# Keys' weights behind the first loads, x scaled on VectorE, block products' weights at shifting offsets

## Chip, core and metric

The kernel runs on one NeuronCore of a Trainium2 chip. The metric is the device time of one execution in microseconds, taken as the median of several runs. TensorE multiplies matrices, VectorE and ScalarE do the elementwise work, GpSimd does a little of it and issues some transfers, and SP (SyncE) issues the other transfers. Each engine works through its own instructions in order.

## Reference

One layer of a hybrid decoder on x of 512 x 1024 float32: a token mixer (HGRN2 and gated DeltaNet side by side, 4 heads of 128) and a SwiGLU feed-forward part.

```python
def hybrid_layer(x, ...):
    u = rms_norm(x, pre_mix_w)
    proj = u @ w_in                       # 512 x 6152
    hg_q, hg_f, hg_i, hg_g, dn_q, dn_k, dn_v, dn_g, dn_a, dn_b, m_a, m_b = split(proj)
    o_a = head_rms_norm(hgrn2_mix(hg_q, hg_f, hg_i, lb), hg_norm_w) * silu(hg_g)
    cq, ck, cv = split(silu(causal_short_conv(concat(dn_q, dn_k, dn_v), conv_w)))
    o_b = head_rms_norm(gated_deltanet_mix(cq, ck, cv, dn_a, dn_b, ...), dn_norm_w) * silu(dn_g)
    merged = sigmoid(m_a) * (o_a @ w_o_hg) + sigmoid(m_b) * (o_b @ w_o_dn)
    h = x + rms_norm(merged @ w_out, post_mix_w)
    gate, up = split(rms_norm(h, pre_ffn_w) @ w_gate_up)      # 2 x 2816
    return h + rms_norm((silu(gate) * up) @ w_down, post_ffn_w)
```

## The kernel before

Every operand of a large product is split into a high part (cast to float32r by ScalarE) and a low part (the rest, a subtraction), and a product is three matmuls: high by high, high by low, low by high. Weights come from memory through `wload`: a transfer of 512 KB on SP's queue into one of two buffers `raw`, a cast on ScalarE into one of three buffers `whi` (L114), a subtraction on VectorE into one of three buffers `wlo` (L115). `wload` runs at high priority.

The order of each engine's instructions is made by a planner, ahead of the run, from priorities and the times that it expects. `high_priority` moves instructions ahead; `issue_after(ins)` puts the instructions of its block behind `ins` where they are on the same engine.

`start` (L195 to L268) comes first. Nine matmuls on a matrix of ones warm TensorE up (L202). Then eight pieces of x transposed (`xT`, L211, 256 KB each) and eight pieces of the weights `w_iab` (L217, 260 KB each) are loaded in pairs, with four pieces of x in rows (L228, 512 KB each) between them. ScalarE multiplies a piece of x by the gains `pmw` into its high part (L218), VectorE makes the low part (L155); the weights are split by a cast (L126) and a subtraction (L152). From these come 192 matmuls (L251) with 256 or 264 columns. The first product uses x before its normalisation; the normalising factor of each token is applied afterwards, and as a row vector, copied to all partitions, it is `rbc` (L267).

`mixers` (L756) follows. The keys' projection `dn_k` (four `wload`s, 96 matmuls of 512 columns, L122 and L123) also uses the unnormalised operand. `normalise` (L270) makes the operands of all later projections: a GpSimd product of x and `rbc` (L277), a ScalarE activation with the gains (L278), a VectorE operation for the low part (L279). Each head of the keys passes a short convolution on VectorE (`conv_evac`). `gates` makes small tables and sends them through memory by GpSimd's queue. Then comes `hg_f`, the forget gate's projection, the first that reads the normalised operand; the column sums of the keys (L392, L393) are set between its matmuls.

The feed-forward part makes 14 of its 22 column blocks by seven half-size products each (`winograd`, `product`, L1086 to L1088): 84 matmuls of 256 columns a block, with moving operands made once and weights made by `operand` from sums of weight blocks. Two such weights share one buffer of `whi` and one of `wlo`, one in each half. `out_proj` and the down projection work with 512 columns.

The tag `st` has three buffers. They hold the states of the two recurrences, then the two halves of `pre_ffn_w` (L918), then those of `post_ffn_w` (L1213). Their loads are on GpSimd's queue, which also carries the stores of the merge gate `m_a` (`early_a`, L826).

Of the kernel before, what the change touches and what calls it, by code (L numbers as in the profile page):

```python
# [9 lines left out]
F32 = mybir.dt.float32  # L10
F32R = mybir.dt.float32r
BF16 = mybir.dt.bfloat16
U32 = mybir.dt.uint32
AF = mybir.ActivationFunctionType
ALU = mybir.AluOpType

P = 128
# [4 lines left out]
NH = 4  # L22
# [2 lines left out]
EPS = 1e-6  # L25
NEG = -30000.0
FIRST, PACE = 8, 5
PADS = (96, 48)
HG_LEVELS = (64, 32, 16, 8, 4, 2, 1)
HG_MASKS = (16, 8, 4, 2, 1)  # L30

# [14 lines left out]
class K:  # L46
    def __init__(self, ctx, nc, tc, I, out):
        self.nc, self.tc, self.I, self.out = nc, tc, I, out
        e = ctx.enter_context
        self.cp = e(tc.tile_pool(name="cp", bufs=1))  # L50
        self.wp = e(tc.tile_pool(name="wp", bufs=1))
        self.bp = e(tc.tile_pool(name="bp", bufs=1))
        self.tp = e(tc.tile_pool(name="tp", bufs=1))
        self.dp = e(tc.tile_pool(name="dp", bufs=1, space=bass.MemoryType.DRAM))
        self.ps = e(tc.tile_pool(name="ps", bufs=1, space=bass.MemoryType.PSUM))
        self.n = self.ncol = self.nraw = 0
        self.log = {}


# [16 lines left out]
        return self.tp.tile([P, 512], F32, tag="out", name=self.name("out"), bufs=1)  # L76

    def st(self):
        return self.tp.tile([P, NH, P], F32, tag="st", name=self.name("st"), bufs=3)

    def sm(self, shape, bufs=1):
        nm = self.name("sm")
# [22 lines left out]
    def wload(self, src, shape):  # L105

        nc = self.nc
        n = shape[1] * shape[2]
        with self.tc.high_priority():
            raw = self.wp.tile([P, 1024], F32, tag="raw", name=self.name("raw"), bufs=2)  # L110
            hi = self.wp.tile([P, 1024], F32R, tag="whi", name=self.name("whi"), bufs=3)
            lo = self.wp.tile([P, 1024], F32R, tag="wlo", name=self.name("wlo"), bufs=3)
            nc.sync.dma_start(out=raw[:, :n], in_=src)
            nc.scalar.copy(hi[:, :n], raw[:, :n])  # L114
            nc.vector.tensor_tensor(out=lo[:, :n], in0=raw[:, :n], in1=hi[:, :n].bitcast(F32),  # L115
                                    op=ALU.subtract)
        r = lambda t: t[:, :n].rearrange("p (a b) -> p a b", a=shape[1])
        return r(hi), r(lo)

    def mm3(self, ps, lh, ll, rh, rl, start, stop):  # L120
        mm = self.nc.tensor.matmul
        return [mm(ps, lh, rh, start=start, stop=False), mm(ps, lh, rl, start=False, stop=False),  # L122
                mm(ps, ll, rh, start=False, stop=stop)]  # L123
# [34 lines left out]
    def consts(self):  # L158
        nc, I = self.nc, self.I
        nc.scalar.preload_act_table_set("natural_log_exp_and_others")  # L160

        self.pads = [self.cp.tile([P, n], F32, name=f"pad{i}") for i, n in enumerate(PADS[:1])]
        self.onesr = self.cp.tile([P, P], F32R, name="onesr")
        self.first = nc.vector.memset(self.onesr.bitcast(F32), 1.0)

        ncm = 3 + len(HG_MASKS)
        self.cm = self.cp.tile([P, ncm, P], F32, name="cm")
        self.ident, self.triu, self.negm = (self.cm[:, i, :] for i in range(3))
        self.hgm = {h: self.cm[:, 3 + i, :] for i, h in enumerate(HG_MASKS)}
        self.one = self.cp.tile([P, 1], F32, name="one")  # L170
        nc.vector.memset(self.one, 1.0)
        self.eps = self.cp.tile([P, 1], F32, name="eps")
        nc.vector.memset(self.eps, EPS)
        self.lnqs = self.cp.tile([P, 1], F32, name="lnqs")
        nc.vector.memset(self.lnqs, -0.5 * math.log(128.0))
        self.pmw = self.cp.tile([P, KD], F32, name="pmw")
        nc.gpsimd.dma_start(out=self.pmw, in_=I["pre_mix_w"])
        self.pads.append(self.cp.tile([P, PADS[1]], F32, name="pad1"))
        self.cw = self.cp.tile([P, 12, 4], F32, name="cw")
        self.hnw = self.cp.tile([P, 1], F32, name="hnw")  # L180
        self.dnw = self.cp.tile([P, 1], F32, name="dnw")
        self.albc = self.cp.tile([P, 2, 4], F32, name="albc")
        self.lbraw = self.cp.tile([P, 4], F32, name="lbraw")

# [10 lines left out]
    def start(self):  # L195

        nc, I = self.nc, self.I
# [9 lines left out]
        pw = lambda k: self.pmw[:, k:k + 1]  # L207
        for k in range(KD):
            g, j = k // 4, k % 4
            x_, h_, l_ = xr[g][:, j, :], uhi[g][:, j, :], ulo[g][:, j, :]  # L210
            nc.sync.dma_start(out=x_, in_=I["xT"][k])  # L211

            if k % 3 == 0:
                W = [self.slot(j, [P, 3, 640], dt)
                     for j, dt in zip(((15, 0, 3), (4, 1, 13), (15, 2, 14))[k // 3], (F32, F32R, F32R))]
            raw, hi, lo = (w[:, k % 3, :520] for w in W)
            nc.sync.dma_start(out=raw, in_=I["w_iab"][k // 2, :, k % 2 * 520:k % 2 * 520 + 520])  # L217
            A.activation(h_, x_, AF.Copy, scale=pw(k))  # L218
            self.stt(l_, x_, pw(k), h_.bitcast(F32), ALU.mult, ALU.subtract)
            self.split(hi, lo, raw)  # L220
            ws.append((hi, lo))
            if k == 3:
                nc.sync.dma_start(out=self.cm[:, 0:1], in_=I["cmat"][:, 0:1])
            if k >= 3 and k < 7:
                c = k - 3
                if c % 2 == 0:
                    xt.append(self.slot(11 + c // 2, [P, 2, D]))
                nc.sync.dma_start(out=xt[-1][:, c % 2, :], in_=I["x"][c])  # L228
# [14 lines left out]
        for k in range(KD):  # L243
            wh, wl = ws[k]
            st, sp = k == 0, k == KD - 1
            for c in range(NC_):
                ts = slice(c * P, c * P + P)
                uh, ul = uhi[k // 4][:, k % 4, ts], ulo[k // 4][:, k % 4, ts]
                for o, ns, s0 in ((pa[c // 2][:, c % 2 * 256:c % 2 * 256 + 256], slice(0, 256), c % 2 == 0),
                                  (pb[c][:, :264], slice(256, 520), True)):  # L250
                    mm = lambda l, r, **kw: nc.tensor.matmul(o, l, r, skip_group_check=True, **kw)  # L251
                    mm(uh, wh[:, ns], start=st and s0, stop=False)
                    mm(uh, wl[:, ns], start=False, stop=False)
                    mm(ul, wh[:, ns], start=False, stop=sp)
# [15 lines left out]
    def normalise(self):  # L270

        self.xhi = [self.slot(i, [P, 4, S], F32R) for i in range(2)]
        self.xlo = [self.slot(2 + i, [P, 4, S], F32R) for i in range(2)]
        for k in range(KD):
            g, j = k // 4, k % 4
            x, h, pw = self.xr[g][:, j, :], self.xhi[g][:, j, :], self.pmw[:, k:k + 1]
            self.tt(x, x, self.rbc, ALU.mult, self.nc.gpsimd)  # L277
            self.nc.scalar.activation(h, x, AF.Copy, scale=pw)  # L278
            self.stt(self.xlo[g][:, j, :], x, pw, h.bitcast(F32), ALU.mult, ALU.subtract)  # L279


    def small_hg(self):
# [473 lines left out]
    def mixers(self):  # L756
        nc = self.nc
# [1 line left out]
        cm = lambda t: (lambda h, ps: A.copy(t[:, :, h, :], ps.rearrange("p (c t) -> p c t", c=NC_)))  # L759
        run = lambda g: [None for _ in g]  # L760
        self.kT = self.slot(11, [P, NH, S])
        self.dense_in("dn_k", self.conv_evac(self.kT, 4, self.rbc), self.u)
        self.normalise()
        with self.tc.issue_after(self.lasta.ins), self.tc.issue_after(self.lastv.ins):
            self.gates()
# [48 lines left out]
        for c in range(NC_):  # L814
            n = self.dn_step(c)
# [46 lines left out]
        for c in range(NC_):  # L862
# [3 lines left out]
            n = self.hg_step(c, at[c])  # L866
# [122 lines left out]
    def operand(self, src):  # L989

        if self.half is None:
            self.half = [self.wp.tile([P, 1024], F32R, tag=t, name=self.name(t), bufs=3) for t in ("whi", "wlo")]
            o = [t[:, :512] for t in self.half]
        else:
            o = [t[:, 512:1024] for t in self.half]
            self.half = None
        self.split(o[0], o[1], src)
        return o
# [179 lines left out]
    def down(self):  # L1178
# [18 lines left out]
        def prod(ps, a, w, c, st, sp, n=slice(0, 512), off=0):  # L1197
            ts = slice(c % 2 * P, c % 2 * P + P)
            gh, gl = a[:, 0, ts], a[:, 1, ts]
            cols = slice(off + n.start, off + n.stop)  # L1200
            T.matmul(ps[:, n], gh, w[0][:, cols], start=st, stop=False, skip_group_check=True)
            T.matmul(ps[:, n], gh, w[1][:, cols], start=False, stop=False, skip_group_check=True)
            T.matmul(ps[:, n], gl, w[0][:, cols], start=False, stop=sp, skip_group_check=True)
# [148 lines left out]
```

## Time and profile before

| | us |
|---|---|
| median of three runs | 841.11 |
| the three runs | 837.80, 841.11, 843.64 |
| the profiled execution | 839.1 |
| its span | 837.3 |
| TensorE busy | 813.8 |
| VectorE busy | 587.0 |
| ScalarE busy | 491.4 |
| GpSimd busy | 99.3 |

The span is the time from the first to the last instruction on the core; the execution's own time has some overhead around it. Times in the rows below count from the start of the span. PE is TensorE, DVE VectorE, ACT ScalarE, POOL GpSimd and SP SyncE; PEclk is the share of the full TensorE clock that was granted.

### The profile page before, as it was taken

What the parts mean: (1) busy time and instruction counts of PE and PEld (TensorE: products, weight loads), DVE (VectorE), ACT (ScalarE), POOL (GpSimd) and SP (SyncE); (2) the same over time, 40 slices, a digit from 0 to 9 for tenths busy, and PEclk for the clock granted to TensorE, in tenths of its full rate; (3) what the DMA queues carried; (4) which work ended last, traced back from release to release, by engine and by line L of the source; (5) the groups of instructions that cost most, each with busy time, mean ns of one, the idle gap of its engine ahead of it and who ended that gap; (6) DMA issues with size and microseconds to landing.
All of it is one profiled execution on the core that took longest, in us unless ns stands there. A gap on an engine that the chain in (4) does not pass through costs nothing.

```text
span 837.3 us, 12305 instructions
## 1 busy us (share of the span) xinstructions
PE 813.8 (97%) x4677; PEld 691.0 (83%) x4677; DVE 587.0 (70%) x935; ACT 491.4 (59%) x917; POOL 99.3 (12%) x138
## 2 busy tenths in 40 slices
PE   7998999999999999999999999999999999999995
PEld 6986888866887878888888999999999998876764
DVE  4497899734747898953855898787778778547554
ACT  4657897966567566676544455455455457545543
POOL 1051068500020000023100300000000000000000
PEclk8999999999999999999999999999999999999999
DMA  8416343632225121467212213422422405556553
GB/s 265 191 50 202 112 141 101 170 101 77 76 88 177 49 77 48 130 238 248 82 49 94 70 52 101 151 59 93 151 72 81 151 26 176 174 178 200 181 173 100
DMA packets 36442, 103.76 MB, mean 124 GB/s; under 512 B 4448, under 2 KB 4864, under 8 KB 36256
## 3 DMA queue, kind: packets, MB, share of 16 engines
q1 hardware_dynamic: 32112, 88.65, 32.0%
q0 software_dynamic: 4272, 14.33, 5.7%
q8 instruction: 36, 0.59, 0.3%
q14 instruction: 22, 0.18, 0.1%
HBM read 94.57 MB, written 8.40 MB: 123 GB/s over the span
## 4 chain that ended last, share of the span: by engine, by line
PE 75%; DMA 11%; DVE 8%; ACT 4%; issue 1%; SPq 0%; DVEq 0%; ACTq 0%
PE mm L122 24%; PE mm L123 12%; DMA raw<-in_w_down_dram 9%; DVE wlo L115 4%; PE hps L122 3%; ACT whi L114 3%; PE hps L1087 2%; PE hps L1086 2%; PE hps L1088 2%; PE hps L700 2%; DVE s L155 2%; PE hps L123 2%; PE dps L1087 2%; PE dps L1088 2%; PE dps L1086 2%; PE mm L1087 2%
## 5 line engine op out<-in xcount | busy, mean ns | idle before, releaser
L122 PE MATMUL mm<-s,whi 128*128 128x512 f32 (+1 forms) x992 | 313.8, 390 | 1.4 <-DVE s L155 1.4
L122 PEld LDWEIGHTS mm<-s,whi 128*128 128x128 f32 x992 | 182.4, 189 | 36.3 <-DVE s L155 2.2
L115 DVE TENSOR_TENSOR wlo<-raw,whi 128x1024 fp32r<-128x1024 f32 x108 | 134.1, 1241 | 98.7 <-ACT whi L114 97.0
L123 PE MATMUL mm<-s,wlo 128*128 128x512 f32 (+1 forms) x496 | 192.0, 387 | 0.0
L114 ACT CAST whi<-raw 128x1024 fp32r<-128x1024 f32 x108 | 113.1, 1047 | 70.1 <-DMA raw<-in_w_down_dram 34.6
L123 PEld LDWEIGHTS mm<-s,wlo 128*128 128x128 f32 x496 | 93.5, 189 | 15.9
L152 POOL TENSOR_TENSOR s<-s,dct 128x512 f32<-128x512 f32 (+1 forms) x9 | 13.1, 1494 | 395.5 <-DVE s L155 360.0
L126 ACT CAST whi<-s 128x512 fp32r<-128x512 f32 x42 | 25.9, 616 | 50.2 <-PE mm L122 20.0
L126 ACT CAST whi<-raw 128x512 fp32r<-128x512 f32 x56 | 34.0, 616 | 28.3 <-PE mm L1087 10.4
L1086 PE MATMUL hps<-s,whi 128*128 128x256 f32 x168 | 47.6, 283 | 0.4 <-DVE hct L152 0.4
L1087 PE MATMUL hps<-s,whi 128*128 128x256 f32 x168 | 47.6, 284 | 0.0
L1088 PE MATMUL hps<-s,wlo 128*128 128x256 f32 x168 | 47.5, 283 | 0.0
L122 PE MATMUL hps<-s,whi 128*128 128x512 f32 (+1 forms) x144 | 40.6, 367 | 0.0
L152 DVE TENSOR_TENSOR wlo<-raw,whi 128x512 fp32r<-128x512 f32 x56 | 37.9, 688 | 2.2 <-ACT whi L126 1.2
L152 POOL TENSOR_TENSOR s<-s 128x126 f32<-128x126 f32 (+22 forms) x62 | 33.4, 538 | 8.3 <-DMA s<-scr 3.5
L1086 PEld LDWEIGHTS hps<-s,whi 128*128 128x128 f32 x168 | 32.2, 192 | 0.8 <-DVE hct L152 0.6
L1087 PEld LDWEIGHTS hps<-s,whi 128*128 128x128 f32 x168 | 32.2, 192 | 0.4 <-DVE s L152 0.2
L152 DVE TENSOR_TENSOR s<-s,s 128x512 f32<-128x512 f32 (+2 forms) x43 | 30.2, 713 | 3.0 <-ACT s L126 2.7
L1088 PEld LDWEIGHTS hps<-s,wlo 128*128 128x128 f32 x168 | 32.2, 192 | 0.0
L1088 PE MATMUL mm<-s,wlo 128*128 128x256 f32 x112 | 31.7, 283 | 0.0
L1087 PE MATMUL mm<-s,whi 128*128 128x256 f32 x112 | 31.7, 283 | 0.0
L1086 PE MATMUL mm<-s,whi 128*128 128x256 f32 x112 | 31.7, 283 | 0.0
(318 smaller groups left out, 1832.4 us busy)
## 6 DMA issues: line engine op xcount, KB each, us to landing
raw<-in_w_in_a_dram SPq DMA_DIRECT2D x44, 512.0 KB, 3.5
raw<-in_w_down_dram SPq DMA_DIRECT2D x44, 512.0 KB, 3.4
s<-in_w_gu_dram SPq DMA_DIRECT2D x56, 256.0 KB, 4.2
raw<-in_w_gu_dram SPq DMA_DIRECT2D x16, 512.0 KB, 3.4
raw<-in_w_o_dram SPq DMA_DIRECT2D x8, 512.0 KB, 3.8
dct<-in_w_out_dram SPq DMA_DIRECT2D x16, 256.0 KB, 5.8
s<-in_w_iab_dram SPq DMA_DIRECT2D x8, 260.0 KB, 6.9
s<-in_xT_dram SPq DMA_DIRECT2D x8, 256.0 KB, 7.0
```

The source lines that it names most:

```text
L114: nc.scalar.copy(hi[:, :n], raw[:, :n])
L115: nc.vector.tensor_tensor(out=lo[:, :n], in0=raw[:, :n], in1=hi[:, :n].bitcast(F32), op=ALU.subtract)
L122: return [mm(ps, lh, rh, start=start, stop=False), mm(ps, lh, rl, start=False, stop=False), mm(ps, ll, rh, start=False, stop=stop)]
L123: mm(ps, ll, rh, start=False, stop=stop)]
L126: self.nc.scalar.copy(hi, src)
L152: return (eng or self.nc.vector).tensor_tensor(out=out, in0=a, in1=b, op=op)
L155: self.nc.vector.scalar_tensor_tensor(out=out, in0=a, scalar=s, in1=b, op0=op0, op1=op1)
L700: T.matmul(ps[:, h, :], E[:, h, :], E[:, h, :], start=True, stop=True)
L1086: mm(ps, wh[:, k, :], ah[k], start=start and k == 0, stop=False, skip_group_check=True)
L1087: mm(ps, wh[:, k, :], al[k], start=False, stop=False, skip_group_check=True)
L1088: mm(ps, wl[:, k, :], ah[k], start=False, stop=k == 3, skip_group_check=True)
```

## The change

Three things are done. First, the loads of the four keys' weights are put behind the last load of `w_iab` on SP's queue (`issue_after(self.lastw.ins)`). Second, `normalise` multiplies x by the gains and by `rbc` in one VectorE operation, in place; the high part is then a plain cast on ScalarE and the low part a plain subtraction on VectorE, and GpSimd has no part in it. Third, the buffers `whi` and `wlo` grow from 1024 to 1152 columns, and a pair of buffers that `operand` takes is used from an offset of 16 + 16 o columns, with o from 0 to 6 on its own for `whi` and for `wlo`: 49 pairs for the 49 pairs of buffers of the block products. `st` has two buffers instead of three, the one-column constants share one tile `few`, and the two unused pads (96 and 48 columns) become one of 32.

```diff
-PADS = (96, 48)
+PAD = 32
+WCOLS = 1152
...
     def st(self):
-        return self.tp.tile([P, NH, P], F32, tag="st", name=self.name("st"), bufs=3)
+        return self.tp.tile([P, NH, P], F32, tag="st", name=self.name("st"), bufs=2)
...
-            hi = self.wp.tile([P, 1024], F32R, tag="whi", name=self.name("whi"), bufs=3)
-            lo = self.wp.tile([P, 1024], F32R, tag="wlo", name=self.name("wlo"), bufs=3)
+            hi = self.wp.tile([P, WCOLS], F32R, tag="whi", name=self.name("whi"), bufs=3)
+            lo = self.wp.tile([P, WCOLS], F32R, tag="wlo", name=self.name("wlo"), bufs=3)
...
-        self.one = self.cp.tile([P, 1], F32, name="one")
+        few = self.cp.tile([P, 5], F32, name="few")
+        self.one, self.eps, self.lnqs, self.hnw, self.dnw = (few[:, i:i + 1] for i in range(5))
...
-            nc.sync.dma_start(out=raw, in_=I["w_iab"][k // 2, :, k % 2 * 520:k % 2 * 520 + 520])
+            self.lastw = nc.sync.dma_start(out=raw, in_=I["w_iab"][k // 2, :, k % 2 * 520:k % 2 * 520 + 520])
...
-            self.tt(x, x, self.rbc, ALU.mult, self.nc.gpsimd)
-            self.nc.scalar.activation(h, x, AF.Copy, scale=pw)
-            self.stt(self.xlo[g][:, j, :], x, pw, h.bitcast(F32), ALU.mult, ALU.subtract)
+            self.stt(x, x, pw, self.rbc, ALU.mult, ALU.mult)
+            self.split(h, self.xlo[g][:, j, :], x)
...
-        self.dense_in("dn_k", self.conv_evac(self.kT, 4, self.rbc), self.u)
+        with self.tc.issue_after(self.lastw.ins):
+            self.dense_in("dn_k", self.conv_evac(self.kT, 4, self.rbc), self.u)
...
-            self.half = [self.wp.tile([P, 1024], F32R, tag=t, name=self.name(t), bufs=3) for t in ("whi", "wlo")]
+            offs = (self.pair % 7, self.pair // 7 % 7)
+            self.pair += 1
+            self.half = [self.wp.tile([P, WCOLS], F32R, tag=t, name=self.name(t), bufs=3)[:, 16 + 16 * o:1040 + 16 * o]
+                         for t, o in zip(("whi", "wlo"), offs)]
             o = [t[:, :512] for t in self.half]
         else:
-            o = [t[:, 512:1024] for t in self.half]
+            o = [t[:, 512:] for t in self.half]
```

## Rows read from the trace of the kernel before

**Rows 1.** The page: busy time of TensorE, and its clock by slice

```profile
PE 813.8 (97%) x4677; PEld 691.0 (83%) x4677; DVE 587.0 (70%) x935; ACT 491.4 (59%) x917; POOL 99.3 (12%) x138
...
PEclk8999999999999999999999999999999999999999
```

**Rows 2.** Waits of PE: what waited for whom, total us, times, longest

```profile
PE mm L251 <- ACT s L126: 4.2, 1, 4.2
PE dps L392 <- ACT dct L126: 2.3, 1, 2.3
PE mm L122 <- DVE s L155: 1.4, 2, 1.0
```

**Rows 3.** Chain of waits, 20 to 26 us: start, us, what

```profile
23.23 0.36 PE dps L251 x3
...
24.31 0.46 PE mm L122 x2
```

**Rows 4.** Timeline of SP's queue, 0 to 16 us: start, us, what

```profile
0.74 0.86 SPq L113 DMA_DIRECT2D raw<-in_w_in_a_dram  x2
...
6.88 1.54 SPq L113 DMA_DIRECT2D raw<-in_w_in_a_dram  x2
...
15.26 0.33 SPq L113 DMA_DIRECT2D raw<-in_w_in_a_dram  x1
```

**Rows 5.** Timeline, 0 to 10 us: POOL, ACT and PE; idle before and its releaser

```profile
1.25 0.68 POOL L177 DMA_DIRECT2D pmw<-in_pre_mix_w_dram  x1 [0.80 <-POOLq L1341]
...
4.54 1.05 ACT L114 CAST whi<-raw 128x1024 fp32r<-128x1024 f32 x1 [2.53 <-DMA raw<-in_w_in_a_dram]
...
6.74 0.72 ACT L218 ACTIVATE s<-s,pmw 128x512 fp32r<-128x512 f32 x1
...
8.62 0.62 ACT L126 CAST s<-s 128x520 fp32r<-128x520 f32 x1 [1.16 <-DMA s<-in_w_iab_dram]
...
9.29 0.58 PE L251 MATMUL mm<-s,s 128*128 128x256 f32 x1 [4.20 <-ACT s L126]
```

**Rows 6.** DMA issues, 0 to 40 us: count, KB, us to landing

```profile
pmw<-in_pre_mix_w_dram POOLq DMA_DIRECT2D x1, 4.0 KB, 4.7
```

**Rows 7.** Windows: busy us of each engine, granted clock, DMA share, GB/s

```profile
9.29:15.00 5.71, 5.71 (x23) 5.42 (x24) 3.13 (x4) 2.58 (x4) 0.00 (x0) 0.50 0.99 354
15.00:38.00 23.00, 23.00 (x186) 22.61 (x185) 9.80 (x22) 13.77 (x28) 0.00 (x0) 1.00 0.66 239
...
38.00:58.00 20.00, 20.00 (x95) 16.65 (x94) 17.69 (x21) 13.09 (x29) 11.95 (x8) 1.00 0.08 27
```

**Rows 8.** Timeline, 40 to 54 us: POOL's products and DVE

```profile
40.57 11.95 POOL L152 TENSOR_TENSOR s<-s,dct 128x512 f32<-128x512 f32 x8 [35.47 <-ACT dct L267]
...
40.63 1.25 DVE L155 SCALAR_TENSOR_TENSOR sm<-sm 128x16 f32<-128x16 f32 x1 [0.94 <-ACT sm L317]
...
43.04 0.16 DVE L155 SCALAR_TENSOR_TENSOR sm<-sm,sm 128x16 f32<-128x16 f32 x1
...
51.29 1.78 DVE L155 SCALAR_TENSOR_TENSOR s<-s,pmw,s 128x512 fp32r<-128x512 f32 x1
...
53.65 0.74 DVE L155 SCALAR_TENSOR_TENSOR s<-s,pmw,s 128x512 fp32r<-128x512 f32 x1
```

**Rows 9.** Timeline, 74 to 77 us: ACT, then PE

```profile
74.74 1.04 ACT L114 CAST whi<-raw 128x1024 fp32r<-128x1024 f32 x1 [1.99 <-DMA raw<-in_w_in_a_dram]
...
76.84 0.50 PE L392 MATMUL dps<-dct,onesr 128*128 128x512 f32 x1 [2.30 <-ACT dct L126]
```

**Rows 10.** Timeline of POOL, 340 to 372 us

```profile
358.54 0.54 POOL L1213 DMA_DIRECT2D st<-in_post_ffn_w_dram  x1 [12.25 <-PE dps L735]
361.13 0.55 POOL L826 DMA_DIRECT2D early_a<-out  x1 [2.06 <-ACT out L149]
```

**Rows 11.** Chain of waits, 560 to 566 us, in a block product

```profile
560.50 0.12 PE dps L1087
560.62 0.12 PE dps L1088
```

More of the change, by code (lines that the diff above doesn't have):

```diff
@@ L55, in __init__ @@
         self.ps = e(tc.tile_pool(name="ps", bufs=1, space=bass.MemoryType.PSUM))
-        self.n = self.ncol = self.nraw = 0
+        self.n = self.ncol = self.pair = 0
         self.log = {}
@@ L160, in consts @@
         nc.scalar.preload_act_table_set("natural_log_exp_and_others")
-        self.pads = [self.cp.tile([P, n], F32, name=f"pad{i}") for i, n in enumerate(PADS[:1])]
         self.onesr = self.cp.tile([P, P], F32R, name="onesr")
@@ L169, in consts @@
         self.hgm = {h: self.cm[:, 3 + i, :] for i, h in enumerate(HG_MASKS)}
-        self.one = self.cp.tile([P, 1], F32, name="one")
+        few = self.cp.tile([P, 5], F32, name="few")
+        self.one, self.eps, self.lnqs, self.hnw, self.dnw = (few[:, i:i + 1] for i in range(5))
         nc.vector.memset(self.one, 1.0)
-        self.eps = self.cp.tile([P, 1], F32, name="eps")
         nc.vector.memset(self.eps, EPS)
-        self.lnqs = self.cp.tile([P, 1], F32, name="lnqs")
         nc.vector.memset(self.lnqs, -0.5 * math.log(128.0))
@@ L177, in consts @@
         nc.gpsimd.dma_start(out=self.pmw, in_=I["pre_mix_w"])
-        self.pads.append(self.cp.tile([P, PADS[1]], F32, name="pad1"))
+        self.pad = self.cp.tile([P, PAD], F32, name="pad")
         self.cw = self.cp.tile([P, 12, 4], F32, name="cw")
-        self.hnw = self.cp.tile([P, 1], F32, name="hnw")
-        self.dnw = self.cp.tile([P, 1], F32, name="dnw")
         self.albc = self.cp.tile([P, 2, 4], F32, name="albc")
```

## Prediction

> **What bounds the kernel now.** I read the page first. TensorE is busy for 97% of the span [rows 1], so a change can gain only where TensorE stands still, where its clock is low, or where a matmul takes longer than it must. The second view is the waits of TensorE alone. Its three longest are short and all lie in the first 80 us: 4.2 us for the first split weights, 2.3 us at the first column sum of the keys, 1.4 us in two waits of the forget gate's projection (hg_f) for VectorE [rows 2]. The clock line of the page adds one thing: of its 40 slices only the first is below full clock [rows 1]. So what this change can give back lies before 80 us, with one exception, the block products of the FFN, which I take apart below. The third view is the chain of waits, for the length of a matmul at full clock: three of the first stage's take 0.36 us, two 512-column ones 0.46 [rows 3].
>
> **The start: keys' weights behind the first loads.** Now SP issues two of the keys' loads (512 KB each) ahead of the first piece of x, another pair at 6.88 and the next weights at 15.26 [rows 4]. The later ones wait in SP's queue until one of the two raw buffers is free, and the pieces of x wait behind them. ScalarE casts two keys' weights before it touches x (6.74), waits for the first w_iab piece until 8.62, and TensorE begins at 9.29 [rows 5]. After the change x's first piece and w_iab's first piece head the queue. Together they are 516 KB, about the keys' load that is there at 4.54 now [rows 5], so they should be there at 4.5. But the activation on x also needs the gains pmw, which GpSimd asks for at 1.25 [rows 5] and which land 4.7 later [rows 6]: 5.95. An activation of 0.72 and a cast of 0.62 [rows 5] follow: TensorE begins at 7.3, 2.0 us earlier. Bounds: 4.1 earlier (the cast of w_iab ahead of the activation, 4.54 + 0.62 = 5.2), and 0 (ScalarE keeps its order). I take 2.0, since pmw's landing is a row.
>
> What is moved past what: all four keys' loads now follow the eight pairs of x and w_iab and the four row-major pieces of x; behind them on SP stand 448 KB of masks, first read at the gates, and all later weights. Who waits: the keys' casts on ScalarE and so the 96 keys' matmuls. Ahead of the first keys' load go 8 x 516 + 4 x 512 + 64 KB = 6.4 MB. At 354 GB/s, the rate of 9.29 to 15.00 [rows 7], that is 18 us; with 2 us before and 2 us for the load itself the weights land near 22 and are split by 25. TensorE needs them at 7.3 + 192 x 0.12 = 30.3. At 239 GB/s, the rate of 15 to 38 [rows 7], they would be split at 33: 2.7 us late. I take 0, because the slower rate holds stretches in which SP stood before a full buffer [rows 4], which the change takes away. The keys' matmuls that fill holes of the first stage today are only moved: 0.
>
> **The clock.** From 9.29 to 15.00 the granted clock is 0.50, that is 1.2 GHz, and TensorE is busy all that time: 5.7 us of work at half speed, 2.9 us lost; afterwards it is 1.00, 2.4 GHz [rows 7]. Before it fell, TensorE had warmed up until 5.1 and then stood idle for 4.2 us [rows 2]. After the change the hole is 2.2 us. The nearest row is the idle 2.30 us ahead of 76.84 [rows 9], in slices at full clock [rows 1]. So I take the whole 2.9 back. The other end: the clock falls again and stays down until 15, as it did: from 7.3 that is 7.7 us at half speed, 3.9 lost, 1.0 worse than before. The Trainium skill (TensorE: Matmul & The Clock Gate, Part 1) says that the watch on TensorE's activity runs freely against a kernel's start; by that the same hole could cost nothing in one execution and the clock in the next, and this term would lie at either end. One trace can't show it.
>
> **Scaling x.** Removed: eight GpSimd products, 11.95 us in one row, and with them a slowdown of VectorE that the timeline shows beside it: while GpSimd runs, an operation on 16 elements takes 1.25 us (0.16 alone), one on 512 takes 1.78 (0.74 alone) [rows 8]. Eight operations, from 40.63 to 51.29, are stretched so, by 7.9 us in sum (four small ones by about 1.05 us each, 4.2, and four large ones by 0.5 to 1.1, 3.7). Added: eight VectorE operations with two products in each, at the 0.74 of the same form [rows 8]: 5.9 us. The other eight become plain subtractions: 0. VectorE's work in this stage falls by 2.0 us. That matters, since VectorE is busy for 17.7 of the 20 us from 38 to 58 [rows 7], and hg_f waits for its last low halves. rbc, which starts the scaling, also comes earlier, because the first stage starts earlier and no longer shares TensorE with keys' matmuls. So the two waits, 1.4 us [rows 2], go. Bounds: 0 and 1.4 gained, and a loss in the second rival.
>
> **The column sum.** TensorE stands before 76.84 for a cast on ScalarE. That cast stood behind the cast of a later weight, which waited 1.99 us for its load [rows 9]. That load shared the DMA engines with two transfers of GpSimd's queue (gates and zeros). With VectorE ahead the weight's buffer comes free earlier and its load meets less of them; what the planned order makes of it is not to be seen in this trace. I take the 1.99, and not the whole idle 2.30: the rest is the sum's own cast. Bounds 0 and 2.3.
>
> **The rest.** The block products: 14 blocks x 84 = 1176 matmuls of 256 columns, 0.12 from start to start [rows 11] whichever of the three buffers and two halves holds the weights. As six places give the same distance now, I take 0 for the new offsets; bound 0.01 us each way, the last figure of these rows: 11.8 us in all. The st buffers go from 3 to 2: GpSimd's queue now holds a load of post_ffn_w until 358.54 for the last state product, and the store behind it is ready only at 361.13 [rows 10]. After the change the second pre_ffn_w load takes that wait, and post_ffn_w waits for out_proj, long before the down projection reads it. Cost 0; without that cover the store would be late by what the wait passes 361. The few constants in one tile and the other pads: 0.
>
> **The sum.** 2.0 + 2.9 + 1.4 + 2.0 = 8.3 us. The profiled execution took 839.1 (a span of 837.3 and 1.8 around it), so 830.8; the median of the three runs is 2.0 above it, so 832.8. After 80 us TensorE's work is the same and hardly waits, so what is gained at the start should stay.
>
> **The rivals.** (1) The clock falls again: 2.0 - 1.0 + 1.4 + 2.0 = 4.4, 837. For it: the first hole cost the clock. Against: the hole of 2.30 us did not. (2) VectorE stays the bound. If each step of the scaling waits for ScalarE's copy between its two VectorE operations, eight copies of 0.62 (5.0 us) come on top, and VectorE is 3.0 later than now instead of 2.0 earlier; hg_f and the column sum each wait 3.0 more: 2.0 + 2.9 - 6.0 = -1.1, 842, and with half of the copies waiting 837. Against: VectorE has convolutions to do between them. (3) The offsets cost. Place: the 1176 block matmuls; price 1.18 us for each nanosecond; from 7.1 ns on it eats the whole gain, and at 10 ns it is 11.8 - 8.3 = 3.5 slower, 844.6. Against: six equal places today. The same with a gain of 0.01 us would be 821. (4) The change does not do at the start what it says: casts of the keys keep their place ahead of x in ScalarE's order, or the planned order of the engines, which is made anew, brings a wait of its own: 841, give or take 3. (5) More is gained, the cast comes ahead of the activation and the whole hole at the column sum goes: 8.3 + 2.1 + 0.3 = 10.7, 830.
>
> **How the numbers follow.** Forecast 0.40, (1) 0.18, (2) 0.10, (3) 0.05 slower and 0.03 faster, (4) 0.12, (5) 0.12. Within 1% (8.4 us, about what a measurement of this kernel can tell from no change) lie (1), (2), most of (4) and half of the forecast, which sits on the edge: 0.48. Faster by more: half the forecast, (5), the good side of (3) and a little of (1) and (4): 0.43. Slower: the bad side of (3) and the tail of (4): 0.09. The range leaves out (3) and the ends of (2) and (4): from 827, which is (5) less 3 for the spread of the runs, to 841.
>
> **What would show it.** Start: the first keys' load issued after the last w_iab load, no wait on SP ahead of it, the first L251 matmul near 7.3. Clock: windows from 5 to 16 us at 1.00; a 0.50 among them is rival (1). Scaling: no GpSimd products, no VectorE operation of 16 elements above 0.3 us, no wait of hg_f for VectorE. Column sum: no idle of ScalarE for a w_in load ahead of it. Block products: 0.12 again. The forecast is wrong if the keys' matmuls wait for weights after the first stage, or if a new wait of TensorE above 2 us stands anywhere after 80 us.

## The result, and the profile after

The changed kernel took 850.62 us (median of 4 runs, 848.61 to 853.68), the kernel before 840.13 beside it. The ratio is 1.0124, with a 95% interval of 1.0075 to 1.0174: slower by 10.5 us, where 8.3 less were forecast. A ratio here and below leaves out every run more than 1.5% above the fastest of its kernel (one of 1609.71 us of the kernel before among them), so it need not be the ratio of the two medians. The profiled execution is the longest of the four, 853.68 (span 851.4), 14.6 above the profiled one of before; what is read from rows below is of this pair.

The page of the changed kernel, the engines' busy time and TensorE's clock by slice:

```profile
PE 824.7 (97%) x4677; PEld 696.3 (82%) x4677; DVE 585.4 (69%) x943; ACT 488.5 (57%) x917; POOL 87.3 (10%) x130
...
PEclk9999999966999999999999999999999999999998
```

Busy share and number of matmuls are those of [rows 1]. New are two slices at 0.6, the ninth and tenth: 170 to 213 us. To place the loss I set the start of each matmul beside the start of the same matmul (the n-th of its line) in the trace before. The changed kernel leads by 3.5 us at the first matmul, 4.1 in the keys' projection, 8.3 from 106 to 155 us. At 212 us it is 15.1 behind, and it ends 14.1 behind. So a gain of the forecast size was there, 8.3, and then 23.4 us were lost in less than 60 us. That the gain met the forecast to the tenth is luck: its terms were off both ways, as the part on the prediction shows.

The start of the changed kernel: ACT, PE and SP by time, with the idle time before them (answers to [rows 4, 5]):

```profile
4.52 0.72 ACT L215 ACTIVATE s<-s,pmw 128x512 fp32r<-128x512 f32 x1 [2.50 <-DMA pmw<-in_pre_mix_w_dram]
...
5.81 0.58 PE L248 MATMUL mm<-s,s 128*128 128x256 f32 x1 [0.54 <-ACT s L127]
...
16.29 1.00 SPq L114 DMA_DIRECT2D raw<-in_w_in_a_dram  x2
```

Its windows (busy us of PE, PEld, DVE, ACT, POOL with their counts, clock, DMA share, GB/s; answers to [rows 7]):

```profile
5.81:10.50 4.69, 4.69 (x21) 4.69 (x22) 3.53 (x6) 3.09 (x5) 0.00 (x0) 1.00 0.89 266
10.50:16.00 5.50, 5.50 (x48) 5.50 (x47) 2.70 (x5) 3.36 (x7) 0.00 (x0) 1.00 1.04 408
38.00:58.00 20.00, 20.00 (x90) 16.59 (x89) 19.94 (x29) 8.19 (x12) 0.00 (x0) 1.00 0.30 94
...
184.00:208.00 24.00, 24.00 (x141) 14.98 (x140) 3.83 (x4) 8.94 (x22) 0.84 (x2) 0.51 0.20 67
```

Its waits of PE, the longest three of the work proper (answers to [rows 2]; of the waits there 0.54 of the first is left, see the row at 5.81, and none of the others):

```profile
PE dps L491 <- DMA s<-scr: 4.6, 1, 4.6
PE dps L388 <- ACT dct L127: 3.0, 1, 3.0
PE dps L491 <- ACT dct L506: 1.7, 1, 1.7
```

The first waits for GpSimd's loads (L491 is `dn_inv`, a chain of small products), the second is at the query's last column sum (L388), the third is in `dn_inv` again, for copies by ScalarE. With 0.45 more at that column sum, for its low half, TensorE stood for 9.7 us between 156 and 183. The other 13.7 of the 23.4 are matmuls that stand farther apart, nearly all of them where the granted clock is 0.50 (1.2 GHz): from 160.7 to 164.1, 170.9 to 177.7 and 184.6 to 208.5. In the last stretch TensorE is never idle. It runs `dn_inv`'s small products between projection matmuls, the same kind of work that the kernel before ran at full clock:

```profile
184.00:208.00 24.00, 24.00 (x170) 16.02 (x170) 8.11 (x12) 13.34 (x32) 1.08 (x2) 1.00 0.22 75
```

**Where it comes from.** `dn_inv` needs the inverse of the 32-wide blocks, which GpSimd works out (62 operations), stores (scr) and loads again. GpSimd's queue, first before:

```profile
102.62 0.89 POOL L442 DMA_DIRECT2D scr<-s  x1 [2.30 <-DVE s L152]
...
112.45 38.16 POOL L152 TENSOR_TENSOR s<-s 128x31 f32<-128x31 f32 x62 [3.51 <-DMA s<-scr]
...
158.69 0.66 POOL L499 DMA_DIRECT2D s<-scr  x1 [3.10 <-DMA scr<-s]
...
164.22 0.57 POOL L795 DMA_DIRECT2D early_q<-out  x1 [0.89 <-ACT out L794]
```

and after:

```profile
109.36 0.89 POOL L438 DMA_DIRECT2D scr<-s  x1 [10.10 <-DVE s L153]
...
121.42 37.25 POOL L153 TENSOR_TENSOR s<-s 128x31 f32<-128x31 f32 x62 [5.38 <-DMA s<-scr]
...
167.63 0.66 POOL L495 DMA_DIRECT2D s<-scr  x1 [2.94 <-DMA scr<-s]
...
170.93 0.57 POOL L792 DMA_DIRECT2D early_q<-out  x1
```

The inverse starts 9.0 us later, though TensorE is ahead. Its input, the second store of the decayed key products, waits 10.10 us for VectorE. The key matmuls themselves ended 2.4 us earlier than before. VectorE's last key product, before and after:

```profile
101.64 0.69 DVE L152 TENSOR_TENSOR s<-dps,dct 128x512 f32<-128x512 f32 x1
```

```profile
108.39 0.68 DVE L153 TENSOR_TENSOR s<-dps,dct 128x512 f32<-128x512 f32 x1
```

It is VectorE's 110th operation before and the 131st after. Of the 21 more, 8 are the products of the new scaling, 9 belong to the query's convolutions and 3 are low halves of later weights. The first `early_q` store (the first quarter of `hg_q`, spilled to memory) stands behind the inverse's loads in GpSimd's queue, and the spill buffer `out`, out of which it is stored, exists once. So ScalarE, ready for the second copy, stands still:

```profile
158.57 0.58 ACT L791 COPY out<-mm 128x512 f32<-128x512 f32 x1
...
177.54 0.58 ACT L791 COPY out<-mm 128x512 f32<-128x512 f32 x1 [10.74 <-DMA early_q<-out]
```

Behind that copy in its order are the copies (L506) that `dn_inv`'s next products need. In the kernel before GpSimd was free only 0.89 us before that store was due (its row at 164.22).

### The profile page after: what moved, and what is told of

The parts are those of the page before. It is cut to its first block, busy times and chain, and to the rows that moved or that the text cites. A ratio compares the mean times of both kernels' runs of the same rounds, so it can differ in the third digit from the quotient of the medians.

```text
span 851.4 us, 12291 instructions
## 1 busy us (share of the span) xinstructions
PE 824.7 (97%) x4677; PEld 696.3 (82%) x4677; DVE 585.4 (69%) x943; ACT 488.5 (57%) x917; POOL 87.3 (10%) x130
## 4 chain that ended last, share of the span: by engine, by line
PE 68%; DMA 11%; issue 7%; DVE 5%; POOL 5%; ACT 3%; DVEq 0%; ACTq 0%; POOLq 0%
PE mm L123 19%; PE mm L124 9%; DMA raw<-in_w_down_dram 8%; POOL s L153 4%; PE hps L123 3%; DVE wlo L116 3%; PE hps L1088 2%; PE hps L1087 2%; ACT whi L115 2%; PE hps L1089 2%; PE hps L696 2%; PE mm L942 2%; PE mm L940 2%; PE mm L941 2%; PE hps L124 2%
## 5 line engine op out<-in xcount | busy, mean ns | idle before, releaser
L123 PE MATMUL mm<-s,whi 128*128 128x512 f32 (+1 forms) x992 | 320.8, 399 | 0.0
L123 PEld LDWEIGHTS mm<-s,whi 128*128 128x128 f32 x992 | 186.4, 193 | 35.9 <-issue 0.7
L124 PE MATMUL mm<-s,wlo 128*128 128x512 f32 (+1 forms) x496 | 196.0, 395 | 0.0
L124 PEld LDWEIGHTS mm<-s,wlo 128*128 128x128 f32 x496 | 95.9, 193 | 16.8 <-DVE wlo L116 0.5
L127 ACT CAST whi<-raw 128x512 fp32r<-128x512 f32 x56 | 34.0, 617 | 27.6 <-PE mm L1088 10.2
L153 DVE TENSOR_TENSOR s<-s,s 128x512 fp32r<-128x512 f32 (+2 forms) x51 | 35.6, 710 | 3.2 <-ACT s L127 2.9
L127 ACT CAST s<-s 128x512 fp32r<-128x512 f32 (+1 forms) x32 | 19.8, 619 | 25.1 <-DVE s L153 16.8
L153 POOL TENSOR_TENSOR s<-s 128x126 f32<-128x126 f32 (+22 forms) x62 | 32.5, 524 | 10.2 <-DMA s<-scr 5.4
L1087 PE MATMUL mm<-s,whi 128*128 128x256 f32 x112 | 31.5, 282 | 0.0
```

The source lines that it names most:

```text
L127: self.nc.scalar.copy(hi, src)
L153: return (eng or self.nc.vector).tensor_tensor(out=out, in0=a, in1=b, op=op)
L1087: mm(ps, wh[:, k, :], ah[k], start=start and k == 0, stop=False, skip_group_check=True)
```

## The experiments

All ratios are against the kernel before, run beside it on the same chip. Theory A is the chain above, from the late inverse to the half clock; its rivals stand in the expectations.

**The start alone** (scaling and places as before).

```diff
+            self.lastw = nc.sync.dma_start(out=raw, in_=I["w_iab"]...
+        with self.tc.issue_after(self.lastw.ins):
             self.dense_in("dn_k", ...
```

> Only the loads are requeued and the keys' projection follows the last w_iab load; GpSimd still scales x, and the block products keep their places. Theory A (the loss comes from the order of VectorE's and ScalarE's work that goes with the new scaling: the last chunk's decay late, GpSimd's inverse 9 us late, TensorE waits in front of dn_inv and runs at half clock after it): here the four key products stand in VectorE's order where they stood before, so GpSimd's inverse starts near 112 us or a few us earlier, TensorE waits at dn_inv for at most 1 us, the clock falls for at most 4 us, and 3 to 5 us of the 6.6 us lead at the end of the first stage are kept: 835 to 838. Theory B (TensorE runs ahead of ScalarE and meets dn_inv too early, whatever the order): the lead of the first stage alone is enough, the wait at dn_inv is over 3 us, the clock stays low until about 208 us, 845 to 850.

830.0 us, ratio 0.9905 [0.9885, 0.9926]: 1% faster. Its GpSimd queue and its window over `dn_inv`:

```profile
105.63 38.27 POOL L152 TENSOR_TENSOR s<-s 128x31 f32<-128x31 f32 x62 [3.79 <-DMA s<-scr]
...
157.11 0.57 POOL L796 DMA_DIRECT2D early_q<-out  x1 [0.60 <-ACT out L795]
```

```profile
160.00:198.00 38.00, 38.00 (x295) 25.16 (x293) 13.94 (x20) 22.59 (x51) 2.18 (x4) 1.00 0.28 96
```

The order of VectorE up to the key products is that of before, so the inverse moves forward with TensorE, by 6.8 us, and a lead of 7.1 is kept to 690 us. Theory B falls: being 7.1 us early costs nothing here. The start was worth more than theory A said (835 to 838).

**The scaling alone.**

```diff
-            self.tt(x, x, self.rbc, ALU.mult, self.nc.gpsimd)
-            self.nc.scalar.activation(h, x, AF.Copy, scale=pw)
-            self.stt(self.xlo[g][:, j, :], x, pw, h.bitcast(F32), ...
+            self.stt(x, x, pw, self.rbc, ALU.mult, ALU.mult)
+            self.split(h, self.xlo[g][:, j, :], x)
```

> Only the scaling of x moves from GpSimd to VectorE. Theory A: the four key products stand in VectorE's order as late as in the changed kernel, so GpSimd's inverse starts at about 121 us or later instead of 112.45; TensorE is only some 3 us ahead, so it waits 1 to 4 us at dn_inv, the first early_q store is issued only after GpSimd's loads, and the clock falls to 0.50 for 10 us or more: 842 to 850. Theory B: without the earlier start TensorE does not come too early: no wait at dn_inv, the two gains of hg_f and the column sum stay, 836 to 838.

858.26 us is the median of four runs, 845.44, 857.74, 858.79 and 860.55; the ratio, 1.0155 [1.0080, 1.0231], rests on the first two of these. The profiled run (857.74) leads by 5.4 us at 152 and trails by 20.9 at 227. GpSimd and ScalarE:

```profile
122.47 36.90 POOL L152 TENSOR_TENSOR s<-s 128x31 f32<-128x31 f32 x62 [4.16 <-DMA s<-scr]
...
172.10 0.57 POOL L794 DMA_DIRECT2D early_q<-out  x1
```

```profile
177.47 0.59 ACT L793 COPY out<-mm 128x512 f32<-128x512 f32 x1 [10.99 <-DMA early_q<-out]
```

The key products are VectorE's operations 112, 116, 121 and 128; in the whole change they are 114, 115, 119 and 131, before 102, 103, 105 and 110. So the scaling brings the late inverse; the loss was larger than expected.

**All but the places** (start and scaling; three st buffers).

> Start and scaling as in the changed kernel, block products at the places of before and three st buffers. Theory A and B: all of the loss stays, and with it the same waits at the query's last column sum (3.0 us) and at dn_inv (4.6 us) and the clock at 0.50 until about 208 us; the block products stand 120 ns apart again instead of 118, so 2 us slower than the changed kernel: 852 to 854. Theory C (the new places, or the store and load of the two st buffers, cost the time): 831 to 834.

848.33 us, ratio 1.0124 [1.0107, 1.0141]. TensorE waits 3.9, 3.2 and 3.0 us in the same places; the last stretch at 0.50 is shorter here, 180.8 to 197.8, and the time lies below the 852 to 854 expected. Theory C falls. The 2 us that the places give in the block products are less than these runs vary.

**`dn_inv` met later.**

```diff
-        last = self.dn_inv((self.log["hg_q"] + self.log["hg_g"])[51::3])
+        last = self.dn_inv((self.log["hg_q"] + self.log["hg_g"])[87::2])
```

> The changed kernel, but dn_inv's 28 groups of products are set after every second matmul from the 88th of hg_q and hg_g on instead of every third from the 52nd, so TensorE meets the first of them 36 matmuls, 8.2 us, later and the last of them 2 us later. Theory A and B: no wait for GpSimd's loads, ScalarE is not held by the early_q store, the clock stays at 1.00 but for the 3.4 us after the query's last column sum, whose wait of 3.0 us stays: lead over the kernel before near 3 us at 212 us, 831 to 835. Theory D (only the idle time counts, and the clock falls whenever the small 32-column products come thin between large ones): the 6.3 us of waits go, the half-clock stretch stays, 843 to 846.

862.65 us, ratio 1.0285 [1.0270, 1.0300]: a miss for theory A as it stood. The wait for the loads is gone, but a longer one has come, PE first, then ACT:

```profile
185.89 0.63 PE L491 MATMUL dps<-s,s 32*32 32x32 f32 x8 [9.99 <-ACT dct L506]
```

```profile
177.16 0.59 ACT L791 COPY out<-mm 128x512 f32<-128x512 f32 x1 [10.48 <-DMA early_q<-out]
```

It is ScalarE, held by the spill buffer, that TensorE then waits for. The theory became A2: the late inverse hurts above all through the store behind it.

**The stores from ScalarE's queue**, alone, and with `[87::2]`.

```diff
             A.copy(t, ps)
-            nc.gpsimd.dma_start(out=early_q[i], in_=t)
+            nc.scalar.dma_start(out=early_q[i], in_=t)
```

> The changed kernel, but the four early_q stores are issued by ScalarE right behind the copy that fills the one spill buffer, instead of by GpSimd behind the inverse's stores and loads. Theory A2 (the late inverse hurts above all through GpSimd's queue: the store stands behind it, ScalarE's next copy waits for the spill buffer, and the copies that dn_inv needs stand behind that): ScalarE's wait of 10.7 us and TensorE's 1.7 us go, the waits of 3.0 and 4.6 us stay with a few us of half clock after each, and the stretch at 0.50 from 184 to 208 us does not come: 836 to 840. Theory D (the small 32-column products between large ones lower the clock by themselves once a wait has come before them): the stretch stays, 847 to 851.

> Both: early_q stores from ScalarE, and dn_inv's groups from the 88th matmul of hg_q and hg_g on. Theory A2: the 10.0 us wait of the run with the later groups alone was ScalarE held by the store; here nothing waits at dn_inv, only the query's column sum (3.0 us and 3.4 us of half clock) is left: 830 to 834. If that 10.0 us wait had another cause (copies of dn_inv too far back in ScalarE's order): 845 to 863.

Alone: 849.70 us, ratio 1.0135 [1.0110, 1.0159]; both: 828.53, ratio 0.9876 [0.9853, 0.9899]. With both edits nothing waits at `dn_inv` and the clock holds over the whole of it, though the groups are closer there:

```profile
168.00:202.00 34.00, 34.00 (x285) 22.61 (x284) 15.05 (x23) 22.41 (x51) 3.68 (x5) 1.00 0.38 125
```

A2 stands: the 34 us between this run and the one with `[87::2]` alone hang on the queue of four stores, with the planned order that goes with it (TensorE's differs from 186 us on). The store alone was a miss. ScalarE is not held by it any more, but TensorE still waits 5.9 us for the loads, and the clock then did what theory D said:

```profile
178.00:193.90 15.90, 15.90 (x152) 11.44 (x151) 3.75 (x4) 9.72 (x26) 0.00 (x0) 0.98 0.32 102
193.90:215.00 21.10, 21.10 (x86) 13.35 (x84) 5.63 (x9) 7.25 (x15) 0.57 (x1) 0.50 0.08 31
```

TensorE had not been idle since 171.4. The new planned order has 27 projection matmuls in a row and then the held-up groups close together, with no more than four projection matmuls between them; behind that the clock falls to 0.50 at 193.3. A wait is thus not the only way down.

**The decays ahead** of the query's convolutions, in a block of higher priority.

```diff
+        with self.tc.high_priority(offset=3000):
+            lms = [self.dn_decay(c) for c in range(NC_)]
...
+        with self.tc.high_priority(offset=3000):
             self.tt(self.B[:, c], ps, lm, ALU.mult)
```

> The changed kernel, but the four chunks' decays for the key products are put ahead of the query's convolutions, and the four products too: the last one stands 7 places earlier in VectorE's order (18 places later than before the change until now, 11 left). Theory A (order): GpSimd's inverse starts 4 to 6 us earlier than 121.4, its loads land before TensorE comes or at most 1 us after, the early_q store is issued 4 to 6 us earlier, so ScalarE is held 5 us instead of 10.7: most of the loss comes back, 832 to 840. Theory B (TensorE is simply too early): 846 to 851.

846.11 us, ratio 1.0081 [1.0054, 1.0108]. By the ratios that is some 3.6 us better than the change, not the 11 to 19 expected: the inverse came 2.8 us earlier, not 4 to 6, and the store 3.3. GpSimd, then PE:

```profile
118.62 36.54 POOL L153 TENSOR_TENSOR s<-s 128x31 f32<-128x31 f32 x62 [6.48 <-DMA s<-scr]
...
167.62 0.57 POOL L794 DMA_DIRECT2D early_q<-out  x1
```

```profile
181.55 0.63 PE L493 MATMUL dps<-s,s 32*32 32x32 f32 x8 [8.10 <-ACT dct L508]
```

The wait for the loads is gone, the one behind the store is not (ScalarE is held for 9.9 us). It agrees with A2: the last key product is now VectorE's operation 124, 7 places earlier, and the inverse comes earlier, but not by enough to spare the hold.

**One place for the weights.** In the changed kernel the block matmuls stand 111 to 124 ns apart, start to start, mean 117.6, against 119.9 before [rows 11]. Sorted by the place of the high and the low weights (the address in bytes modulo 256), those at 0 and 128 stand 113.9 apart on average, those at 64 and 128 stand 119.6. The next run has the start alone, with that best pair for the block products and for the projections. It and the later ones of this kind are made from the changed kernel, with GpSimd's scaling put back (those lines are left out here):

```diff
-            offs = (self.pair % 7, self.pair // 7 % 7)
-            self.pair += 1
-            self.half = [self.wp.tile(...)[:, 16 + 16 * o:1040 + 16 * o] for t, o in zip(("whi", "wlo"), offs)]
+            self.half = [self.wp.tile(...)[:, o:o + 1024] for t, o in zip(("whi", "wlo"), (16, 48))]
...
-            hi = self.wp.tile([P, WCOLS], ...)
+            hi = self.wp.tile([P, WCOLS], ...)[:, 16:1040]   # lo [:, 48:1072]
```

> The start alone (GpSimd scales x as before), and all split weights of the projections and of the block products at one place: high halves from column 16, low halves from column 48 of their buffers, that is 0 and 128 bytes past a multiple of 256, the pair at which the changed kernel's block products stood 113 to 114 ns apart. Theory P (the place within 256 bytes sets the distance): 1176 block matmuls 6.5 ns closer than at 120, 7.6 us; and if the 512-column matmuls of the projections follow by the same 6.5 ns, some 1200 of them, another 7 us: 815 to 823. Rival (the distances of the changed kernel come from its changing places, not from a good one): 0.12 again, 829 to 831.

829.29 us, ratio 0.9884 [0.9849, 0.9919], as the start alone. The block products did as theory P said, 113 or 114 ns for 1113 of 1176. But the projections' 512-column matmuls went from 227.8 ns on average to 231.8, some 5.5 us over 1359 of them, most of what the blocks gave. So a place that is good at 256 columns is bad at 512.

Each load of the projections at another pair, the blocks at the good one:

```diff
+            a, b = 16 * (self.pair % 4), 16 * (self.pair // 4 % 4)
+            self.pair += 1
-            hi = self.wp.tile([P, WCOLS], ...)
+            hi = self.wp.tile([P, WCOLS], ...)[:, a:a + 1024]   # lo with b
```

> As the start with the block products at one place, but each weight load of the projections takes the next of 16 pairs of places (multiples of 64 bytes past the buffers' starts). One look at the distances of 512-column matmuls by pair: Theory P expects a fixed distance for each pair, with some pairs below 226 and some above 230; if only a change of place disturbs them, all lie together. Time 822 to 830.

834.96 us, one run. At the place that they have in the changed kernel (192 and 192) the projections' matmuls stand 228.1 ns apart on average; the 15 other pairs lie between 229.3 and 233.0. The distance goes with the pair, but none is better than the old one, and the forecast of pairs below 226 fails. The time holds more than the places: TensorE waits 0.9 us in `dn_inv` here too, and the clock is 0.50 from 172.5 to 182.8.

The pair alone does not tell the whole. The changed kernel's smaller constants move every buffer by 192 bytes modulo 256, that of the moving operands too. In the kernel before all lie at 0, and the blocks stand 119.9 apart; in the changed kernel, with moving operands at 192, weights at 0 and 0 give 117.5, and weights at 192 and 192 give 119.8. That fits a distance set by where the weights lie against the moving operands; no run varied it alone.

The run of the one place, with the projections' weights back at the start of their buffers:

```diff
-            hi = self.wp.tile([P, WCOLS], ...)[:, 16:1040]   # lo [:, 48:1072]
+            hi = self.wp.tile([P, WCOLS], ...)
```

> The start alone, the block products at the one place of the run before (0 and 128 bytes past a multiple of 256), the projections' weights back at the start of their buffers. If the place acts on each matmul by itself, both halves of that run come apart: 113 to 114 ns for the 1176 block matmuls, 7 us less than the start alone, and 226 to 227 ns again for the projections instead of 231 to 236: 822 to 824. If the projections there were slower for another reason, their distances stay above 230 and the time stays near 829.

Blocks at the good place, projections at the old: both halves come apart as expected, 113.7 and 227.7 ns, and the blocks give 6.4 us against the start alone. Yet the median is 840.13. Its 12 runs fall into two groups, four at 828.9 to 831.0 and eight at 837.7 to 844.8 (the ratio, 0.9960 [0.9924, 0.9995], is that of the nine shorter ones). The profiled run, of the second group, shows the chain again, from a store only 4 us later than in the start alone: POOL, ACT, PE, and the window behind them:

```profile
161.10 0.57 POOL L793 DMA_DIRECT2D early_q<-out  x1
```

```profile
168.02 0.58 ACT L792 COPY out<-mm 128x512 f32<-128x512 f32 x1 [4.47 <-DMA early_q<-out]
```

```profile
170.51 1.10 PE L492 MATMUL dps<-s,s 32*32 32x32 f32 x16 [3.48 <-ACT dct L507]
```

```profile
174.00:200.00 26.00, 26.00 (x131) 16.13 (x129) 3.84 (x4) 7.98 (x19) 1.08 (x2) 0.50 0.15 51
```

TensorE's order in `dn_inv`, small groups and projection matmuls between them, is here the same as in the start alone. The same-matmul comparison with the start alone goes from 0.7 us behind at 162 us to 16.7 behind at 203: a wait of 3.5 us cost 16 us, the rest of it by the clock.

The run with everything at one place, above, is a measure for this: each engine's operations stand there in the same order as in the last run. ScalarE is held for 1.9 us in it, TensorE waits 0.9, and the clock stays at 1.00 from 160 to 198. Its wait:

```profile
PE dps L492 <- ACT dct L507: 0.9, 1, 0.9
```

So with one order the loss goes with a longer hold by the same store. The wait's length alone does not set the price: the 0.9 us of the run with 16 pairs of places was followed by 10.2 us at half clock.

**The two fastest versions.** The whole change with `[87::2]`, the stores from ScalarE and the blocks at the one place; and the run just shown with the stores from ScalarE. The edits are those of the diffs above.

> The whole change, with the early_q stores from ScalarE, dn_inv's groups from the 88th matmul on, and the block products at the one place instead of 49 pairs. Theory A2: as the run with both edits (828.5), less 1176 matmuls by some 4 ns: 823 to 825. If that run was fast by the luck of one planned order, 830 to 850.

> The start, the block products at the one place, and the early_q stores from ScalarE. The run without the last edit fell into two groups, 829 to 831 and 838 to 845, and its profile shows ScalarE held 4.5 us by the first store, TensorE waiting 3.5 us behind that and then half clock. If that is the cause, the hold is gone in every execution, the runs lie within 3 us of each other, and the place keeps its 6.5 us against the start alone: 822 to 826. If the two groups come from something else (the chip's clock by itself, the place), they stay: some runs at 838 to 845.

824.43 us, ratio 0.9842 [0.9828, 0.9856]; 823.59 us, ratio 0.9821 [0.9802, 0.9841], its five runs within 1.8 us of each other. The first has the same order of every engine's operations as the run with both edits, so it does not test whether that order was lucky; the second, from another base, does. In its five runs the second group of the run before is gone with the hold of ScalarE, which makes the hold its cause, though the planned order behind 161 us is a new one here too. The chain of waits in a block product, first the changed kernel's, then this last one's:

```profile
560.57 0.12 PE hps L1087
560.69 0.12 PE hps L1088
560.80 0.12 PE hps L1089
```

```profile
560.07 0.11 PE hps L1086
560.18 0.11 PE hps L1087
560.29 0.11 PE hps L1088
```

## Why the prediction was wrong

**The start: right, and undersized.** x's first piece and w_iab's head the queue and the keys' loads follow, and no keys' matmul waits for weights. TensorE begins at 5.81, not 7.3: the gains pmw were there by 4.52, not 5.95. The term is 3.5 us instead of 2.0.

**The clock: the term that could lie at either end lay near the lower one.** In the window from 5.81 the 21 matmuls are 223 ns apart, in the next 115. So TensorE ran at half speed to 10.5, though the clock column says 1.00 there: the trace's first clock record is the rise at 10.50, and ahead of it the column has nothing to go by. 4.7 us at half speed instead of 5.7 is 0.5 us gained of the forecast 2.9. In the start alone TensorE begins at 5.76 and 38 matmuls fit into nearly the same window:

```profile
5.76:10.50 4.74, 4.74 (x38) 4.63 (x39) 3.64 (x6) 2.55 (x4) 0.00 (x0) 1.00 0.91 278
```

That is full speed at once, and 6.1 us of lead in the keys' projection where the changed kernel has 4.1. The Trainium skill (TensorE: Matmul & The Clock Gate, Part 1) says that the watch on the activity is not tied to a kernel's start; by that the same start may meet either level, and these two traces agree. The row that the term was taken from, an idle 2.30 us at full clock, was no safe one: in the start alone an idle 1.63 us at the same column sum is followed by 0.50 from 68.95 to 72.36.

**Scaling and column sum: right.** No GpSimd products, small VectorE operations at 0.17 us, hg_f's waits and the wait at the first column sum gone: the lead grows from 4.1 to 8.3, 4.2 us against 3.4. VectorE is busy for 19.94 of the 20 us from 38 to 58 all the same: it takes other work earlier. So the terms came to 3.5, 0.5 and 4.2 where 2.0, 2.9 and 3.4 were forecast, and it is luck that the sums agree.

**The step that failed** is "After 80 us TensorE's work is the same and hardly waits, so what is gained at the start should stay". TensorE's work was the same; what had to be ready for it was not. In its place the runs showed waits of 9.7 us at the query's last column sum and in `dn_inv`, and 13.7 us of half clock behind them, which come with the new scaling (the scaling alone has them, with 1.8, 5.2 and 1.5 us of waits in the same places; the start alone has not). The prediction looked at TensorE's waits alone and gave GpSimd's queue no slack to compare. The row at 164.22 had it: 0.89 us between the issue of the inverse's loads and the store that frees ScalarE's buffer. The query's last column sum had to wait too, for ScalarE, which was busy without a gap from 150 to 155 us in the changed kernel (ACT's 5.00, with 11 operations):

```profile
150.00:155.00 5.00, 5.00 (x23) 4.13 (x22) 2.91 (x5) 5.00 (x11) 4.37 (x9) 1.00 0.15 26
```

The prediction's own sign of being wrong, a new wait above 2 us after 80 us, came true twice (4.6 and 3.0). Rival (4), a planned order with a wait of its own, named the mechanism at 841, give or take 3: a loss of some 8 us instead of 23.4. The 9.7 us of waits by themselves would have fitted it; the half clock behind them was not priced.

**The places: wrong in kind, right in size.** They were put at 0 because six places gave the same 120 ns. The six were equal modulo 256 bytes, so they were one place. The 49 pairs gave about 2 us (1176 by 2.3 ns is 2.7), inside the bound. Two `st` buffers instead of three cost nothing that shows: the run with three has the same ratio, 1.0124.

**Open.** Why the planner puts the key products back when the scaling moves was not taken apart further than the two single edits. What pulls the clock down in the sparse products, the wait or the thin mix, is not settled: a fall was seen behind waits and once without one. Why a pair of places is fast at 256 columns and slow at 512 is not known. That the query's column sum is limited by ScalarE was read, not tried.

## What to carry to other kernels

When an engine that bounds is made to run ahead, list for each thing that it will meet how long that thing was ready before: a queue in order (here GpSimd's, with a slack of 0.89 us) and a buffer that exists once turn a delay of a few us on an idle engine into a wait on the busy one. Where the busy one then runs small, sparse products, price the wait with the half clock that can follow it: 3.5 us of wait cost 16 here. Try a store that frees a buffer on the queue of the engine that fills the buffer: here its issue took 0.33 to 0.35 us of ScalarE's queue. It is no cure alone, where another wait is left: the store moved by itself gained nothing (ratio 1.0135 against 1.0124).

## What the runs showed of the hardware

- The same mix of eight 32-column products and three 512-column matmuls runs at 1.00 where the clock was up (before, start alone) and at 0.50 for 24 us where it had fallen, TensorE busy throughout in both.
- The distance of float32r matmuls depends on the places of the weights modulo 256 bytes: at 256 columns 113.6 to 119.9 ns on average, at 512 columns 227.7 to 233.0, with different best pairs; the moving operands lay at one place in each kernel.
- Ahead of a trace's first clock record the clock column says 1.00 where the distances say half speed (5.81 to 10.50 of the changed kernel, whose first record is the rise at 10.50): count the matmuls of a window too.
- Waits of 0.9 us ahead of the same products were followed by 1.00 in one run (everything at one place) and by 10.2 us at 0.50 in another (16 pairs of places).
